# Down projection of an encoder layer: seven products of sums of blocks on half of the row pairs

## The chip, the core and the metric

The kernel runs on one core of a Trainium2 chip. The time is device microseconds (us) of that core for one execution. The engines are TensorE (PE, matrix products, with its weight loads shown as PEld), VectorE (DVE), ScalarE (ACT), GpSimd (POOL) and SyncE (SP). SP issues the transfers of weights here; ACT and POOL can issue transfers too. SBUF is the core's working memory of 128 partitions, PSUM holds the sums of products in 8 banks of 128x512 floats, HBM is the memory outside the core.

## The reference

One layer of an encoder, for one sequence of 256 tokens, model width 2048, inner width 8192, all in float32. Only its last part changes:

```python
    x = x + rms_norm(y, norm_mix_post[l])
    h = rms_norm(x, norm_mlp_pre[l])
    u = jnp.square(jax.nn.relu(jnp.einsum('bsd,df->bsf', h, w_up[l])))
    x = x + rms_norm(jnp.einsum('bsf,fd->bsd', u, w_down[l]), norm_mlp_post[l])
```

The down projection is the second einsum: u (256 x 8192) times w_down (8192 x 2048). Before it come a projection of 10240 columns, two kinds of attention, two branch projections, gates and an output projection, then the up projection, which is the first einsum.

## The kernel before, in words

**Arithmetic.** TensorE works on a 32-bit type that keeps fewer bits than float32. So each operand is split into two parts, high and low: ACT casts the value to the high part, DVE subtracts the high part from the value, which gives the low part. A product is three products on PE: high by high, high by low, low by high.

**Order of work.** The code is written for a scheduler that builds each engine's order from a simulated timeline of all instructions, priorities following the order in which the code is written; `tc.issue_after` adds an order by hand. A buffer is taken from a pool of fixed count; an instruction that needs a buffer waits until the last reader of the tile that held it is done. `pages` has 27 buffers of 4 KB a partition. `wp` has three buffers of 8 KB each for raw weights (tag `raw`), high parts (`hi`) and low parts (`lo`). `tmp` holds temporaries, `mm` and `ms` four PSUM banks each.

**Weights.** `weight` (L119) is `load` (L98, a transfer of 1024 KB on SP's queue) and then `split` (L115 the cast on ACT, L116 the subtraction on DVE, in two pieces of 1024 columns).

**Up projection.** `wgroup` makes 512 columns of u at a time, transposed, in 16 groups. Products are L191 and L192. Each group ends in `u_evac`: `halves` (L254 and L256) adds two halves of a bank, L761 applies relu and the row factor, L762 squares. The groups stay in SBUF as 16 pages `u0` to `u15`.

**Down projection.** It goes over 64 chunks of 128 rows of w_down, each with all 2048 columns. `dweight` (L750) brings a chunk; when a chunk begins a new group of 512 rows, `usplit` (L743 to L747) splits that page of u into `uh` and `ul`. These are the stationaries, the operands that PE holds while a weight chunk streams past. `dmm` (L772 to L780) makes three products of 512 columns, for each of 2 token tiles and 4 column blocks: 24 products a chunk, 1536 in all, into 8 banks `acc` that stay open over the stage:

```python
        nc.tensor.matmul(acc[t][c], uh[:, k % 4, ts_], hi[:, 0, cs], start=(k == 0), stop=False)
        nc.tensor.matmul(acc[t][c], uh[:, k % 4, ts_], lo[:, 0, cs], start=False, stop=False)
```

The last three chunks are done bank by bank. After each bank ACT squares it with a row sum (L807) and DVE multiplies it by the gain (L809). After four banks come the reduction (L811), the inverse root mean square in `inv_rms` (L85 on DVE, L88 a power on POOL), the scaling and the residual (L816), and the transfer out (L819).

## Time and profile before

| | |
|---|---|
| time, median of 3 runs | 1397.59 us (1396.96 to 1397.92) |
| span of the profiled execution | 1394.5 us |
| the median less that span | 3.1 us |
| mean granted TensorE clock | 0.995 |
| the down projection's products | 1536, from 1037.40 to 1385.60 us |
| HBM read, written | 261.92 MB, 3.92 MB |

The profile gives one execution, on the chip. Its own time is the span, from the first to the last instruction. A row of windows reads: the stretch, its length, then the busy time and the count of instructions of PE, PEld, DVE, ACT and POOL, the mean granted PE clock, the mean busy share of the 16 transfer engines and the GB/s they moved. A group's row reads: line, engine, operation, output and inputs, tile shape, count, then busy time and mean ns of one, then the idle time before it and what ended most of that. In the chain of waits a row has a time, a length, the engine and what it worked on.

### The profile page before, as it was taken

To read this page: it belongs to the slowest core of one execution; us is meant where nothing else is said; L and a number is where in the kernel's file an instruction comes from. 1 tells how busy PE (TensorE), PEld (TensorE's weight loads), DVE (VectorE), ACT (ScalarE), POOL (GpSimd) and SP (SyncE) were. 2 spreads that over 40 slices of the span, in tenths; PEclk is the share of its full clock that TensorE was granted. 3 is DMA by queue.
4 is the path that set the end of the run, shared out by engine and by line. 5 is a ranking of instruction groups with operands and counts; after the bars stand their busy time and mean duration, and the time that the engine had idled before them with its cause. 6 is when DMAs were issued, how large, how long until landed. Compare 5 with 4: busy or idle time off the path is not lost.

```text
span 1394.5 us, 17896 instructions
## 1 busy us (share of the span) xinstructions
PE 1374.6 (99%) x7240; PEld 1177.8 (84%) x7240; DVE 835.8 (60%) x1155; ACT 668.7 (48%) x1023; POOL 7.9 (1%) x19
## 2 busy tenths in 40 slices
PE   7999999999999999999899999999999999999997
PEld 6888888888888888888788888888888888888886
DVE  6868866676656565654755555555575554444445
ACT  7554554545444445543744444444464543334332
POOL 0000000000000000000000000000000000000000
PEclk9999999999999999999999999999999999999999
DMA  9674755564555555675455565656555556555551
GB/s 317 202 214 154 202 177 173 171 191 155 165 205 182 203 181 183 203 279 184 149 182 181 182 193 170 211 170 200 189 196 185 203 186 227 195 187 205 181 199 73
DMA packets 117490, 265.16 MB, mean 190 GB/s; under 512 B 15008, under 2 KB 16288, under 8 KB 109216
## 3 DMA queue, kind: packets, MB, share of 16 engines
q1 hardware_dynamic: 117264, 264.03, 57.3%
q8 instruction: 56, 0.92, 0.3%
q14 instruction: 26, 0.21, 0.0%
q10 hardware_dynamic: 144, 0.01, 0.0%
HBM read 261.92 MB, written 3.92 MB: 191 GB/s over the span
## 4 chain that ended last, share of the span: by engine, by line
PE 98%; DVE 1%; DMA 0%; ACT 0%; SPq 0%; issue 0%; DVEq 0%; POOLq 0%; POOL 0%; ACTq 0%
PE u_p L191 17%; PE u_p L192 9%; PE acc L779 8%; PE acc L778 8%; PE acc L777 8%; PE gb_p L191 4%; PE ga_p L191 4%; PE qa_p L191 2%; PE gb_p L192 2%; PE ga_p L192 2%; PE ka_p L191 2%; PE qn_p L191 2%; PE bb_p L191 2%; PE ba_p L191 2%; PE kn_p L191 2%; PE y_p L229 2%
## 5 line engine op out<-in xcount | busy, mean ns | idle before, releaser
L191 PE MATMUL u_p<-h2T,u_h 128*128 128x512 f32 x1024 | 359.9, 398 | 0.5 <-DVE r_m L85 0.5
L192 PE MATMUL u_p<-h2T,u_l 128*128 128x256 f32 x1024 | 284.3, 280 | 0.0
L116 DVE TENSOR_TENSOR d_l<-d_w,d_h 128x1024 fp32r<-128x1024 f32 x128 | 151.1, 1221 | 164.2 <-ACT d_h L115 163.7
L116 DVE TENSOR_TENSOR u_l<-u_w,u_h 128x1024 fp32r<-128x1024 f32 x128 | 151.1, 1222 | 146.0 <-ACT u_h L115 144.7
L191 PEld LDWEIGHTS u_p<-h2T,u_h 128*128 128x128 f32 x1024 | 192.0, 189 | 45.5 <-DVE r_m L85 0.9
L115 ACT CAST d_h<-d_w 128x1024 fp32r<-128x1024 f32 x128 | 128.3, 1052 | 191.1 <-PE acc L779 187.5
L778 PE MATMUL acc<-d_l,uh 128*128 128x512 f32 x512 | 199.0, 389 | 0.0
L779 PE MATMUL acc<-d_h,ul 128*128 128x512 f32 x512 | 198.9, 389 | 0.0
L777 PE MATMUL acc<-d_h,uh 128*128 128x512 f32 x512 | 198.2, 389 | 0.0
L192 PEld LDWEIGHTS u_p<-h2T,u_l 128*128 128x128 f32 x1024 | 193.8, 189 | 1.3
L115 ACT CAST u_h<-u_w 128x1024 fp32r<-128x1024 f32 x128 | 128.0, 1049 | 123.9 <-PE u_p L191 62.5
L778 PEld LDWEIGHTS acc<-d_l,uh 128*128 128x128 f32 x512 | 96.1, 188 | 20.1
L777 PEld LDWEIGHTS acc<-d_h,uh 128*128 128x128 f32 x512 | 96.1, 188 | 20.0
L779 PEld LDWEIGHTS acc<-d_h,ul 128*128 128x128 f32 x512 | 96.1, 188 | 19.8
L191 PE MATMUL gb_p<-hT,gb_h 128*128 128x512 f32 x256 | 90.4, 398 | 0.0
L191 PE MATMUL ga_p<-hT,ga_h 128*128 128x512 f32 x256 | 90.0, 397 | 0.0
L192 PE MATMUL gb_p<-hT,gb_l 128*128 128x256 f32 x256 | 71.4, 281 | 0.0
L192 PE MATMUL ga_p<-hT,ga_l 128*128 128x256 f32 x256 | 70.3, 280 | 0.0
L191 PEld LDWEIGHTS gb_p<-hT,gb_h 128*128 128x128 f32 x256 | 47.9, 188 | 11.5
L116 DVE TENSOR_TENSOR gb_l<-gb_w,gb_h 128x1024 fp32r<-128x1024 f32 x32 | 37.8, 1221 | 31.1 <-ACT gb_h L115 31.1
L191 PEld LDWEIGHTS ga_p<-hT,ga_h 128*128 128x128 f32 x256 | 47.4, 188 | 10.5
L116 DVE TENSOR_TENSOR y_l<-y_w,y_h 128x1024 fp32r<-128x1024 f32 x32 | 37.9, 1222 | 27.8 <-ACT y_h L115 27.8
(213 smaller groups left out, 2348.1 us busy)
## 6 DMA issues: line engine op xcount, KB each, us to landing
u_w<-in_w_up SPq DMA_DIRECT2D x64, 1024.0 KB, 5.4
d_w<-in_w_down SPq DMA_DIRECT2D x64, 1024.0 KB, 4.9
ga_w<-in_w_in SPq DMA_DIRECT2D x16, 1024.0 KB, 5.2
gb_w<-in_w_in SPq DMA_DIRECT2D x16, 1024.0 KB, 5.2
y_w<-in_w_out SPq DMA_DIRECT2D x16, 1024.0 KB, 5.1
ka_w<-in_w_in SPq DMA_DIRECT2D x8, 1024.0 KB, 6.1
va_w<-in_w_in SPq DMA_DIRECT2D x8, 1024.0 KB, 5.2
qn_w<-in_w_in SPq DMA_DIRECT2D x8, 1024.0 KB, 5.1
```

The costliest lines, as they stand in the source:

```text
L115: nc.scalar.copy(hi[part], raw[part])
L116: nc.vector.tensor_sub(lo[part], raw[part], hi[part].bitcast(F32))
L191: nc.tensor.matmul(ps[b], hi[:, k % 4, cs], mv, start=(k == 0), stop=False)
L192: nc.tensor.matmul(ps[b][:, :T], lo[:, k % 4, cs], mv[:, :T], start=False, stop=(k == nk - 1))
L229: nc.tensor.matmul(ps[t], sh, hi[:, k % 4], start=(k == 0), stop=False)
L777: nc.tensor.matmul(acc[t][c], uh[:, k % 4, ts_], hi[:, 0, cs], start=(k == 0), stop=False)
L778: nc.tensor.matmul(acc[t][c], uh[:, k % 4, ts_], lo[:, 0, cs], start=False, stop=False)
L779: nc.tensor.matmul(acc[t][c], ul[:, k % 4, ts_], hi[:, 0, cs], start=False, stop=(k == NK - 1))
```

## The change

**Stage.** The down projection is done in two halves of 1024 output columns each (g = 0 and 1). The 16 groups of 512 rows of w_down are taken in pairs, and a pair makes a block. A group has four chunks of 128 rows; a chunk goes together with its partner 256 rows further down. So a block has four steps, two of each group, and a step's load is again 1024 KB: 128 rows and their partners, 1024 columns (`down_weights`, L818).

**Seven products.** In the even groups (`seven`) a step is a product of 2 x 2 blocks: two token tiles by two chunks, times two chunks by two column blocks. It is made with seven products of blocks and of sums of blocks in place of eight. Each is still three PE products, so a step has 21. The sums of u's blocks are made once a group (`act_sets`), those of the weights' blocks in each step (L833 to L835), and both are split again. Odd groups (`eight`) do the plain eight, 24 PE products. Plain steps add into banks 1, 2, 3 and 7; banks 0, 4, 5 and 6 belong to the seven products alone. They are emptied and combined into `zw` in the last block of a half (L951 to L955), after that block's second seven-product step; the other four banks are added in `rest` (L892). There are 32 steps of 21 products and 32 of 24, 1440 in all.

**Stationaries.** `act_sets` runs behind each group of the up projection, makes the sums and splits all that the group needs, and POOL writes the parts to HBM (48 transfers). `act_again` reads a pair of groups back, one block ahead, by six transfers on ACT's queue (L791). Two pairs are not read again where they are used next: groups 12 and 13 serve the first block of half 0 straight from the up projection, and groups 14 and 15 stay from the last block of half 0 for the first block of half 1.

**The ends of the halves.** A block's steps alternate between its groups: seven-product step s0, plain n0, then s1, n1. The first block of half 0 has n0, s0, s1, n1. The last block of each half has s0, s1, n0, n1, PE's products there stand in the written order, and the two plain steps are done bank by bank: for each bank its products of both steps, then the addition, the square and, in half 1, the gain. Half 0's gains are written in half 1's seventh block.

The diff, from the pools on, with removed code cut where the listing above shows it:

```diff
-    tmp = ctx.enter_context(tc.tile_pool(name="tmp", bufs=6))
+    temps = ctx.enter_context(ExitStack())
+    tmp = temps.enter_context(tc.tile_pool(name="tmp", bufs=6))
...
-    ust = {}
...
+    NG = DFF // 512
+    kept = {}
+    def seven_of(cg):
+        return cg % 2 == 0
+    def act_sets(cg, u):
+        srcs = []
+        if seven_of(cg):
+            a11, a21 = u[:, 0:2, :P], u[:, 0:2, P:]
+            a12, a22 = u[:, 2:4, :P], u[:, 2:4, P:]
+            sums = page([P, 4, 2, P], F32, f"sm{cg}")
+            nc.vector.tensor_sub(sums[:, 0], a21, a22)
+            nc.vector.tensor_sub(sums[:, 1], a11, a21)
+            nc.vector.tensor_sub(sums[:, 2], sums[:, 0], a11)
+            nc.vector.tensor_add(sums[:, 3], a12, sums[:, 2])
+            srcs = [
+                ([P, 3, 2, P], [(slice(0, 1), u[:, 0:2, :P].unsqueeze(1)),
+                                (slice(1, 3), u[:, 2:4].rearrange("p k (t q) -> p t k q", t=2))]),
+                ([P, 4, 2, P], [(slice(0, 4), sums)]),
+            ]
+        else:
+            srcs = [([P, 4, T], [(slice(0, 4), u)])]
+        got = []
+        for i, (shape, pieces) in enumerate(srcs):
+            hi, lo = page(shape, F32R, f"ah{cg}{i}"), page(shape, F32R, f"al{cg}{i}")
+            for at, src in pieces:
+                nc.scalar.copy(hi[:, at], src)
+                nc.vector.tensor_sub(lo[:, at], src, hi[:, at].bitcast(F32))
+            for n, part in (("h", hi), ("l", lo)):
+                kd = dram.tile(shape, F32, name=f"keep{n}{cg}{i}", tag=f"keep{n}{cg}{i}")
+                nc.gpsimd.dma_start(kd, part.bitcast(F32))
+                kept[cg, i, n] = (shape, kd)
+            got.append([hi, lo])
+        return got
+    def act_again(cg, g):
+        out = []
+        for i in range(2 if seven_of(cg) else 1):
+            got = []
+            for n in "hl":
+                shape, kd = kept[cg, i, n]
+                t = page(shape, F32R, f"b{n}{g}{cg}{i}")
+                nc.scalar.dma_start(t.bitcast(F32), kd)
+                got.append(t)
+            out.append(got)
+        return out
+    sets = {}
+    for cg in range(NG):
         u = page([P, 4, T], F32, f"u{cg}")
...
-        uT.append(u)
-        if cg == DFF // 512 - 2:
-            usplit(0)
...
+        got = act_sets(cg, u)
+        if NG - 4 <= cg < NG - 2:
+            sets[0, cg] = got
+    temps.close()
+    down = ctx.enter_context(tc.tile_pool(name="down", bufs=1, reuse_waits="tile"))
+    wd = a["w_down"].rearrange("(g h j p) c -> p h g j c", h=2, j=2, p=P)
...
+    def down_weights(g, cg, j):
+        raw = wp.tile([P, 4, 512], F32, tag="raw", name=f"dr{g}{cg}{j}")
+        last_load[0] = nc.sync.dma_start(
+            raw.rearrange("p (h b) c -> p h (b c)", h=2),
+            wd[:, :, cg, j, g * 1024 : (g + 1) * 1024],
+        ).ins
+        n = f"{g}{cg}{j}"
+        h1, l1 = wtile("hi", f"dh{n}"), wtile("lo", f"dl{n}")
+        if not seven_of(cg):
+            nc.scalar.copy(h1, raw)
+            nc.vector.tensor_sub(l1, raw, h1.bitcast(F32))
+            return h1, l1
+        t = [page([P, 2, 512], F32, f"dt{n}{i}") for i in range(2)]
+        nc.scalar.copy(h1[:, 1:4], raw[:, 1:4])
+        nc.vector.tensor_add(t[0], raw[:, 1:3], raw[:, 0:1].to_broadcast([P, 2, 512]))
+        nc.vector.tensor_add(t[1][:, 0], t[0][:, 0], raw[:, 2])
+        nc.vector.tensor_add(t[1][:, 1], t[1][:, 0], raw[:, 3])
+        nc.vector.tensor_sub(l1[:, 1:4], raw[:, 1:4], h1[:, 1:4].bitcast(F32))
+        h2 = [down.tile([P, 2, 512], F32R, tag="e", name=f"eh{n}{i}", bufs=4) for i in range(2)]
+        l2 = [page([P, 2, 512], F32R, f"el{n}{i}") for i in range(2)]
+        for i in range(2):
+            nc.scalar.copy(h2[i], t[i])
+            nc.vector.tensor_sub(l2[i], t[i], h2[i].bitcast(F32))
+        return h1, l1, h2, l2
+    class Products:
...
+        def add(self, i, stat, w, blk, last=False):
+            (sh, sl), (wh, wl) = stat, w
+            for n, (st, mv) in enumerate(((sh, wh), (sh, wl), (sl, wh))):
+                with tc.issue_after(self.after) if self.after else nullcontext():
+                    ins = nc.tensor.matmul(
+                        self.ps[i], st, mv[:, blk], start=i not in self.begun, stop=last and n == 2
+                    ).ins
+                self.begun.add(i)
+                if self.in_order:
+                    self.after = ins
+    def seven(pr, sets, j, w, last):
+        def stat(i, at):
+            return tuple(part[:, at, j] for part in sets[i])
+        r, t = w[:2], list(zip(*w[2:]))
+        order = [(0, 0, 0, r, 1), (4, 1, 0, t[0], 0), (6, 1, 1, t[0], 1), (5, 1, 2, t[1], 0)]
+        own = [(2, 1, 3, r, 2), (1, 0, 1, r, 3), (3, 0, 2, t[1], 1)]
+        order = order + own if not pr.begun else order[:1] + own[:2] + order[1:] + own[2:]
+        for i, part, at, ww, blk in order:
+            pr.add(i, stat(part, at), ww, blk, last and i in (0, 4, 5, 6))
+    PLAIN = ((1, 0, 1), (2, 0, 0), (3, 1, 1), (7, 1, 0))
+    def eight(pr, sets, j, w, which, last):
+        i, t, half = PLAIN[which]
+        for k in (0, 2):
+            stat = tuple(part[:, j + k, t * P : (t + 1) * P] for part in sets[0])
+            pr.add(i, stat, w, k + half, last and k == 2)
+    zw = {}
+    ssd = [small(4, f"ssd{t}") for t in range(2)]
+    def rest(g, which, pr):
+        i, t, half = PLAIN[which]
+        z = zw[g, t][:, half]
+        nc.vector.tensor_add(z, z, pr.ps[i])
+        sq = down.tile([P, 512], F32, tag="junk", name=f"jd{g}{which}", bufs=2)
+        c = g * 2 + half
+        nc.scalar.activation(sq, z, AF.Square, accum_out=ssd[t][:, c : c + 1])
+    def gain(g, t, half):
+        z = zw[g, t][:, half]
+        nc.vector.tensor_mul(z, z, gp2[g][:, half * 512 : (half + 1) * 512])
+    def finish(t):
         sd = small(1, f"sd{t}")
-        nc.vector.tensor_reduce(sd, ssd, axis=AX.X, op=ALU.add)
+        nc.vector.tensor_reduce(sd, ssd[t], axis=AX.X, op=ALU.add)
         rd = inv_rms(sd, D, f"rd{t}")
...
+    blocks = [[NG - 4] + list(range(0, NG - 4, 2)) + [NG - 2], [NG - 2] + list(range(0, NG - 2, 2))]
+    for g in range(2):
+        pr = Products(f"p{g}", (0, 4, 5, 6))
+        for bi, b in enumerate(blocks[g]):
+            s0, s1, n0, n1 = (b, 0), (b, 1), (b + 1, 0), (b + 1, 1)
+            end = bi == len(blocks[g]) - 1
+            steps = [n0, s0, s1, n1] if g == 0 and bi == 0 else [s0, n0, s1, n1]
+            if end:
+                steps = [s0, s1, n0, n1]
+                pr.in_order = True
+            ws = {}
+            for n, (cg, j) in enumerate(steps):
+                ws[cg, j] = w = down_weights(g, cg, j)
+                if n == 0 and not end:
+                    for c in range(2):
+                        sets[g, blocks[g][bi + 1] + c] = act_again(blocks[g][bi + 1] + c, g)
+                if n == 0 and end and g == 0:
+                    for c in range(2):
+                        sets[1, b + c] = sets[0, b + c]
+                if g == 1 and bi == 5 and n == 0:
...
+                if g == 1 and bi == 6:
+                    gain(0, n // 2, n % 2)
+                if seven_of(cg):
+                    final = end and n == 1
+                    seven(pr, sets[g, cg], j, w, final)
+                    if final:
+                        for t in range(2):
+                            zw[g, t] = page([P, 2, 512], F32, f"zw{g}{t}")
+                        c11, c12 = zw[g, 0][:, 1], zw[g, 0][:, 0]
+                        c21, c22 = zw[g, 1][:, 1], zw[g, 1][:, 0]
+                        nc.scalar.copy(c11, pr.ps[0])
+                        nc.vector.tensor_add(c12, c11, pr.ps[5])
+                        nc.vector.tensor_add(c21, c12, pr.ps[6])
+                        nc.vector.tensor_sub(c12, pr.ps[4], c12)
+                        nc.vector.tensor_sub(c22, pr.ps[4], c21)
+                elif not end:
+                    for which in range(4):
+                        eight(pr, sets[g, cg], j, w, which, False)
+                elif n == 3:
+                    for which in range(4):
+                        for c, jj in (n0, n1):
+                            eight(pr, sets[g, c], jj, ws[c, jj], which, jj == 1)
+                        rest(g, which, pr)
+                        if g:
+                            gain(1, *PLAIN[which][1:])
+                            if which % 2:
+                                finish(which // 2)
```

**Three places in the order of the instructions.** The first is DVE in a steady block, in the middle of the stage. Before, `d` names are weight chunks (11 to 13 here), `_l`, `_h` and `_w` their low part, high part and raw buffer, `ul` low parts of u:

```order
L747 TENSOR_TENSOR ul9_10399<-u9_7879,uh9_10398 128x1024
L116 TENSOR_TENSOR d11_l_9577<-d11_w_9574,d11_h_9576 128x1024 x2
L116 TENSOR_TENSOR d12_l_9613<-d12_w_9610,d12_h_9612 128x1024 x2
L116 TENSOR_TENSOR d13_l_9645<-d13_w_9642,d13_h_9644 128x1024 x2
L747 TENSOR_TENSOR ul10_10531<-u10_8068,uh10_10530 128x1024
```

In the changed kernel, a block of half 1 with groups 6 and 7 (numbers are half, group, chunk, and a last digit for the sum): `dr` are raw weights, `dt` sums, `dh` and `dl` own high and low parts, `eh` and `el` those of the sums:

```order
L833 TENSOR_TENSOR dt1600_11307<-dr160_11303 128x1024
L836 TENSOR_TENSOR dl160_11306<-dr160_11303,dh160_11305 128x1536
L834 TENSOR_TENSOR dt1601_11308<-dt1600_11307,dr160_11303 128x512
L841 TENSOR_TENSOR el1600_11316<-dt1600_11307,eh1600_11314 128x1024
L835 TENSOR_TENSOR dt1601_11308<-dt1601_11308,dr160_11303 128x512
L828 TENSOR_TENSOR dl170_11358<-dr170_11355,dh170_11357 128x2048
L841 TENSOR_TENSOR el1601_11317<-dt1601_11308,eh1601_11315 128x1024
L833 TENSOR_TENSOR dt1610_11389<-dr161_11385 128x1024
L834 TENSOR_TENSOR dt1611_11390<-dt1610_11389,dr161_11385 128x512
```

Where a chunk had two subtractions, a seven-product step has a subtraction of 1536 columns, three sums and two subtractions of 1024; a plain step has one subtraction of 2048. The rows `ul` are gone from the stage.

The second place is DVE in the last block of half 1, with groups 12 and 13; the first seven-product step is `1120`, the second `1121`, the plain ones `1130` and `1131`:

```order
L835 TENSOR_TENSOR dt11201_11772<-dt11201_11772,dr1120_11767 128x512
L836 TENSOR_TENSOR dl1121_11810<-dr1121_11807,dh1121_11809 128x1536
L841 TENSOR_TENSOR el11201_11781<-dt11201_11772,eh11201_11779 128x1024
L833 TENSOR_TENSOR dt11210_11811<-dr1121_11807 128x1024
L828 TENSOR_TENSOR dl1130_11857<-dr1130_11854,dh1130_11856 128x2048
L834 TENSOR_TENSOR dt11211_11812<-dt11210_11811,dr1121_11807 128x512
L841 TENSOR_TENSOR el11210_11820<-dt11210_11811,eh11210_11818 128x1024
L835 TENSOR_TENSOR dt11211_11812<-dt11211_11812,dr1121_11807 128x512
L828 TENSOR_TENSOR dl1131_11863<-dr1131_11860,dh1131_11862 128x2048
L841 TENSOR_TENSOR el11211_11821<-dt11211_11812,eh11211_11819 128x1024
```

Here the two seven-product steps follow one another, and the low part of the first plain step, `dl1130`, stands ahead of the last three sums and parts of the second seven-product step (`dt11211`, `el11210`, `el11211`).

The third place is DVE in the tail. Before, `zw` are the output rows, `acc` the banks, `gp` the gains, `sd` and `rd` the sums of squares and the inverse roots:

```order
L809 TENSOR_TENSOR zw10_11320<-acc10_9210,gp20_11226 128x512
L816 SCALAR_TENSOR_TENSOR zw00_11255<-zw00_11255,rd0_r_11309,x2_0_5443 128x512 x2
L816 SCALAR_TENSOR_TENSOR zw01_11256<-zw01_11256,rd0_r_11309,x2_1_5444 128x512 x2
L809 TENSOR_TENSOR zw10_11320<-acc11_9211,gp20_11226 128x512
L809 TENSOR_TENSOR zw11_11321<-acc12_9212,gp21_11227 128x512
L809 TENSOR_TENSOR zw11_11321<-acc13_9213,gp21_11227 128x512
L811 TENSOR_REDUCE sd1_11370<-ssd1_11319 128x1
L85 TENSOR_SCALAR rd1_m_11372<-sd1_11370 128x1
```

Now, with `p1` and a digit for the banks of half 1:

```order
L892 TENSOR_TENSOR zw10_11847<-zw10_11847,p12_10689 128x512
L899 TENSOR_TENSOR zw10_11847<-zw10_11847,gp21_11487 128x512
L903 TENSOR_REDUCE sd0_11898<-ssd0_9454 128x1
L86 TENSOR_SCALAR rd0_m_11900<-sd0_11898 128x1
L892 TENSOR_TENSOR zw11_11848<-zw11_11848,p13_10690 128x512
L908 SCALAR_TENSOR_TENSOR zw00_10608<-zw00_10608,rd0_r_11902,x2_0_5443 128x512 x2
L908 SCALAR_TENSOR_TENSOR zw10_11847<-zw10_11847,rd0_r_11902,x2_1_5444 128x512 x2
L899 TENSOR_TENSOR zw11_11848<-zw11_11848,gp21_11487 128x512
L892 TENSOR_TENSOR zw11_11848<-zw11_11848,p17_10694 128x512
L899 TENSOR_TENSOR zw11_11848<-zw11_11848,gp21_11487 128x512
L903 TENSOR_REDUCE sd1_11944<-ssd1_9455 128x1
```

The gain reads the output row in SBUF and no longer the bank; each bank costs DVE an addition and a gain. The four scalings of the first token tile stand ahead of the additions' last, that of bank 7.

More of the change, by code (lines that the diff above doesn't have):

```diff
@@ new lines, in encoder_layer, with __init__ @@
+    class Products:
+        def __init__(self, name, low):
+            self.ps = [bank(f"{name}{i}", i in low) for i in range(8)]
+            self.begun = set()
+            self.after = None
+            self.in_order = False
+        def add(self, i, stat, w, blk, last=False):
[8 more added lines that the diff above has]
+                    self.after = ins
@@ L814, in encoder_layer @@
             cs = slice((c % 2) * 512, (c % 2 + 1) * 512)
-            z = zw[c // 2][:, cs]
+            z = zw[c // 2, t][:, c % 2]
             nc.vector.scalar_tensor_tensor(
```

59 lines of the change are left out of this document (8 added, 51 removed).

## The prediction

> **What bounds the kernel now.** First the page's busy shares and its chain of waits: is one engine the bound from end to end?
>
> ```profile
> PE 1374.6 (99%) x7240; PEld 1177.8 (84%) x7240; DVE 835.8 (60%) x1155; ACT 668.7 (48%) x1023; POOL 7.9 (1%) x19
> PE 98%; DVE 1%; DMA 0%; ACT 0%; SPq 0%; issue 0%; DVEq 0%; POOLq 0%; POOL 0%; ACTq 0%
> ```
>
> TensorE (PE) is 99% busy and 98% of the chain that ended last. Then the stages, by a view of windows: an early stretch of full transfers, a stretch of the up projection, the whole down projection, a stretch of it.
>
> ```profile
> 10.00:20.00 10.00, 10.00 (x55) 8.86 (x54) 7.96 (x13) 9.90 (x21) 0.00 (x0) 1.00 1.05 389
> 900.00:1000.00 100.00, 100.00 (x573) 87.15 (x572) 55.45 (x75) 46.93 (x73) 0.00 (x0) 1.00 0.60 189
> 1037.40:1385.60 348.20, 348.17 (x1536) 287.92 (x1535) 172.13 (x154) 143.65 (x157) 0.54 (x1) 1.00 0.54 187
> 1100.00:1200.00 100.00, 100.00 (x443) 82.78 (x442) 50.30 (x43) 40.84 (x41) 0.00 (x0) 1.00 0.58 201
> ```
>
> The third row is the whole stage that changes: 1536 products in 348.20 us, one every 0.2267 us. (The 389 ns that the groups below give for one product is its latency; products overlap.) VectorE (DVE) is busy half of that time, the transfers a little over half. Last, the groups and waits of the stage show who follows whom:
>
> ```profile
> L778 PE MATMUL acc<-d_l,uh 128*128 128x512 f32 x512 | 199.0, 389 | 0.0
> L116 DVE TENSOR_TENSOR d_l<-d_w,d_h 128x1024 fp32r<-128x1024 f32 x128 | 151.1, 1221 | 164.2 <-ACT d_h L115 163.7
> L115 ACT CAST d_h<-d_w 128x1024 fp32r<-128x1024 f32 x128 | 128.3, 1052 | 191.1 <-PE acc L779 187.5 <-issue 3.6
> SPq L98 <- DVE d_l L116: 290.0, 59, 9.1
> ```
>
> PE is idle for 0.0 us ahead of its products. ScalarE (ACT) waits for PE (a buffer of parts), DVE for ACT, the load queue for DVE: everything waits for PE in the end.
>
> **What is removed.** A step is 128 rows of one half of the output columns with their partner rows 256 further down: 24 products, or 21 where the seven-product form is used. 32 of the 64 steps use it: 96 products fewer, 96 x 0.2267 = **-21.8 us**, if PE stays fed. An estimate from the product rate alone, and the whole of the gain.
>
> **What DVE gets.** The trace has no 1536- or 2048-column subtraction; these rows give its slope:
>
> ```profile
> L256 DVE TENSOR_TENSOR up_s<-u_p,up_r 128x256 f32<-128x256 f32 x64 | 25.4, 419 | 0.0
> L809 DVE TENSOR_TENSOR zw<-acc,gp 128x512 f32<-128x512 f32 x8 | 5.3, 688 | 6.2 <-ACT jd L807 5.9
> L371 ACT CAST n_pT<-n_pt 128x512 fp32r<-128x512 f32 x8 | 4.4, 584 | 0.0
> L98 SPq DMA_DIRECT2D d_w<-in_w_down x19: 327/328/328, 1030.1 to 1128.0; - x19
> ```
>
> 419, 688 and 1221 ns lie on 0.154 + 1.043 ns a column, so 1.76 us for 1536 and 2.29 us for 2048. A seven-step costs DVE 1.22 + 2 x 0.69 + 1.76 + 2 x 1.22 = 6.8 us, a plain one 2.3 us. A block (two of each) is 18.2 us of DVE against 90 x 0.2267 = 20.4 us of PE: 89%, where it is 50% now. ACT by 584 and 1052 ns: 1.5 us for 1536, 2.0 for 2048, so 2 x (1.5 + 2.1) + 2 x 2.0 = 11.2 us, and six issues of 0.33 us (SP's issue, the nearest row): 13.2 us, 65%.
>
> In a steady block I followed the order with these durations. ACT may cast a step's high part when PE has read the buffer three steps back; from there low parts and sums are ready about 7 us before PE's turn. The six DMAs on ACT's queue wait for the last use of the sums two blocks back, which lies ahead of the PE product that the next cast waits for: they stop nothing that would run. Cost 0, hidden by those 7 us; without them, what DVE is late.
>
> At three places the cover is thinner. **Start of the stage:** DVE still has the last evacuation and split of the up projection, and takes the sums of both seven-steps after the low part of the fourth step; against PE's 61 products without sums (13.8 us) four waits of 0.4 to 0.9 us come out: 2 us (bounds 0 and 5). **Last block of each half:** the two seven-steps stand together, and the low part of the third step (which needs a buffer that PE leaves only with its last product of the block before) stands ahead of the second seven-step's last parts. From that product: cast 2.0, low part 2.3, sum 0.7, part 1.2, sum 0.7, low part 2.3, part 1.2 = 10.4 us; PE wants the part 37 products later, at 8.4 us (38 in the first half, 8.6). 2 us late, twice: 4 us (bounds 0 and 8). What is late next is the plain steps, whose parts are ready by then. **Change of halves:** banks 0, 4, 5, 6 are emptied under the 48 plain products of that block (10.9 us); DVE has 12.3 us there: 0.5 us (bounds 0 and 3).
>
> **What the transfers get.** Weights are still 64 loads of 1024 KB, now as 4 KB runs. New are the kept stationaries: 2.88 MB a pair of groups (two of 768 columns, four of 1024), written once for eight pairs (23.1 MB, in the up projection) and read for seven pairs in each half (40.4 MB). A steady block reads 4.19 + 2.88 = 7.08 MB in 20.4 us: 347 GB/s. The first window above moved 389 GB/s over 10 us with several transfers in flight: 18.2 us, so it fits. Share against rate gives other ends: 201 / 0.58 = 347 GB/s for the down weights (20.4 us, just even), 189 / 0.60 = 315 for the up weights' 2 KB runs (22.5 us, 2.1 us a block over 14 blocks: +29 us). I take 0, by the row with transfers side by side, and keep +29 as the bound. A load alone lands in
>
> ```profile
> DMA to landing us min/median/max: 4.7/4.9/6.6
> ```
>
> while the steady order leaves the weights 7 to 13 us between issue and first use, plus PE's 7 us; even behind a whole set, (1.05 + 2.88) MB / 389 = 10.1 us and some 2 us, they arrive.
> The Trainium skill (DMA: Bandwidth & Descriptors, Where 436 GB/s comes from) says that for HBM to SBUF a core's share of the HBM, about 358 GB/s, binds. By it a block would take 19.8 us, still under PE's 20.4, with nothing in reserve; this trace disagrees with its 389 GB/s, and the measurement decides.
>
> **Up projection.** A pair of groups (45 us) gets 4 x 0.42 us of sums and 3584 columns of splits: about 5.7 us on DVE and 4 on ACT, from 55% to 68% and 47% to 55%. Its writes raise 189 GB/s to about 253. POOL, idle, issues them; a page is reused a group or more later, 22 us. I take 0. The trace shows no POOL DMA; bounds 0 and +5 (16 groups, a DVE delay of 0.3 us each that reaches PE).
>
> **The tail.**
>
> ```profile
> 1385.34 0.24 PE acc L779
> 1385.66 0.60 ACT jd L807
> 1386.38 0.69 DVE zw L809
> 1388.05 0.75 DVE zw L816
> ```
>
> Now DVE multiplies after the squares, 1.49 us after PE's end. In the change, four scalings of the first token tile (2.74 us) and a gain stand on DVE ahead of the last bank's addition. From the third bank's addition at -2.7 us: 0.7, 2.7, 0.7, then the addition 0.7 ends at 2.1, squares to 2.8, gain to 3.6 us: **+2.1 us** (bounds 0.8, the addition alone, and 3).
>
> **Sum.** The profiled execution has a span of 1394.5 us; with the 3.1 us around it that the median has over the span it stands at the median, 1397.6. 1397.6 - 21.8 + 2 + 4 + 0.5 + 2.1 = **1384.4**, so 1384 us. With the low ends 1376.6, so the floor is 1376.
>
> **Rivals.**
>
> A. The transfers bind (the other side). Place: the 14 blocks that read stationaries; price above 20.4 us a block. At 315 GB/s: 1384 + 29 = 1413. It decides from 331 GB/s (13.6 / 14 = 0.97 us a block eats the gain). For it: the share of the up weights; against it: 389 GB/s at the start, and 4 KB runs that are nearer the 347 row. 0.10.
>
> B. DVE binds in every block. It has 2.2 us to spare a block, 0.55 a step. Its waits for ACT are now
>
> ```profile
> DVE d_l L116 <- ACT d_h L115: 163.7, 57, 3.1
> ```
>
> 2.9 us each, with nothing else to do. If 1 us a step stays, a block takes 22.2 us: 16 x 1.8 = +29, 1413; slower from 0.8 us a step. Against it: in the order each wait has another step's work ahead of it. 0.08.
>
> C. Waits grow long enough to lower PE's clock. Once in this trace PE waited 3.2 us:
>
> ```profile
> PE h2T_t L664 <- DVE x L657: 3.2, 1, 3.2
> 668.00:672.00 4.00, 1.14 (x5) 0.57 (x4) 2.87 (x9) 3.85 (x13) 0.55 (x1) 0.95 0.00 0
> 672.00:676.00 4.00, 3.15 (x10) 2.46 (x11) 3.88 (x12) 3.10 (x8) 0.54 (x1) 0.50 0.00 0
> 676.00:680.00 4.00, 4.00 (x20) 3.58 (x19) 3.82 (x8) 2.85 (x7) 0.00 (x0) 0.69 0.20 32
> ```
>
> and the granted clock was 0.50 and 0.69 in the next 8 us: 2.0 + 1.2 = 3.2 us more. If the start and both last blocks wait 3.2 us instead of 2, it is 3 x (1.2 + 3.2) = +13: 1397. Mine are 2 us, in pieces. 0.10.
> The Trainium skill (TensorE: Matmul & The Clock Gate, What's actually happening) says the clock halves after an idle window of some 3.4 us; the row agrees, and by that rule waits of 2 us cost no clock.
>
> D. PE is fed throughout and only the tail costs: 1397.6 - 21.8 + 2.1 = 1378. DVE's 89% speaks against it. 0.12.
>
> **Chances.** Forecast (1380 to 1391) 0.60, A 0.10, B 0.08, C 0.10, D 0.12. About 0.2%, 2.8 us, is what a measurement of this kernel can tell. Faster by more: forecast, D, and some of C and of mild A or B: 0.81; same 0.07; slower 0.12. The range 1376 to 1397 takes in D and C and leaves out A and B at their prices.
>
> **What would show it.** Right: 1440 products, 0.226 us each in the middle of the stage; PE idle ahead of products some 6 us in all, ended by DVE parts at the start and in the two last blocks; DVE near 0.89 in steady blocks; about 350 GB/s there; 3.6 us from PE's end to the last gain. Wrong: PE waiting for DMA in steady blocks (A), for DVE in each block (B), or a granted clock under 0.99 in the stage (C).

## The result, and the profile after

The changed kernel takes 1389.77 us (median, 1389.23 to 1390.31), the kernel before 1397.53 us beside it. The ratio is 0.9946, with an interval of 0.9934 to 0.9957: 7.8 us faster, where 13.2 were forecast. It lies inside the range of 1376 to 1397. The profiled execution has a span of 1387.3 us, 7.2 less than the 1394.5 of before, so the accounts below go by the spans.

First the page's busy shares and its chain of waits, then the view of PE's waits over the whole span (in all, times, longest):

```profile
PE 1359.3 (98%) x7144; PEld 1162.4 (84%) x7144; DVE 992.9 (72%) x1315; ACT 720.6 (52%) x1041; POOL 34.0 (2%) x67
PE 95%; DVE 2%; DMA 2%; ACT 1%; issue 0%; SPq 0%; DVEq 0%; POOLq 0%; POOL 0%; ACTq 0%
PE p L858 <- ACT dh L832: 2.7, 1, 2.7
PE p L858 <- DVE el L841: 1.7, 1, 1.7
PE p L858 <- ACT eh L840: 1.3, 2, 0.7
PE p L858 <- ACT dh L827: 0.2, 1, 0.2
```

The last four rows, of `p L858`, are the new waits, all in the down projection: 5.9 us, where about 6 were forecast. Only the 1.7 us end with a DVE part, though; the others end with a cast on ACT. PE has 7144 instructions where it had 7240, 96 fewer. Now windows of 20 us through the stage: the start, a steady stretch, the change of halves, another steady stretch and the end.

```profile
1040.00:1060.00 20.00, 18.68 (x82) 14.85 (x81) 17.41 (x17) 9.77 (x11) 1.07 (x2) 1.00 0.76 280
1060.00:1080.00 20.00, 19.76 (x85) 15.39 (x84) 18.26 (x15) 11.32 (x9) 0.00 (x0) 1.00 1.01 391
1140.00:1160.00 20.00, 20.00 (x90) 16.56 (x89) 17.79 (x15) 11.35 (x9) 0.00 (x0) 1.00 0.92 355
1180.00:1200.00 20.00, 17.29 (x69) 13.79 (x68) 16.15 (x14) 8.74 (x8) 0.00 (x0) 0.91 0.59 211
1240.00:1260.00 20.00, 20.00 (x90) 16.57 (x89) 17.34 (x14) 10.49 (x8) 0.00 (x0) 1.00 1.02 398
1360.00:1380.00 20.00, 14.74 (x57) 11.21 (x55) 13.49 (x22) 3.64 (x10) 0.56 (x1) 0.91 0.15 54
```

The two steady windows hold 90 products, as many as before, with DVE at 0.89 and 0.87 and 355 and 398 GB/s; in the others from 1080 to 1180 us and from 1220 to 1340 us DVE lies between 0.76 and 0.94 and the rate between 307 and 378 GB/s, with no wait of PE. So the middle of the stage is what was forecast. The losses sit in the first two windows, at the change of halves and at the end. The last two places have a granted clock of 0.91.

Where the clock went is seen in windows of 2 us and in PE's timeline there (start, length, and in brackets how long PE was idle ahead and what ended it). First the last block of half 1:

```profile
1360.00:1362.00 2.00, 0.83 (x4) 0.21 (x2) 2.00 (x2) 0.75 (x2) 0.00 (x0) 1.00 0.00 0
1362.00:1364.00 2.00, 1.42 (x4) 1.12 (x5) 0.81 (x2) 0.00 (x0) 0.00 (x0) 0.71 0.04 8
1364.00:1366.00 2.00, 2.00 (x7) 1.51 (x6) 1.93 (x4) 0.00 (x0) 0.00 (x0) 0.50 0.00 0
...
1360.33 0.51 PE L858 MATMUL p<-eh,bh 128*128 128x512 f32 x1
1362.58 0.60 PE L858 MATMUL p<-el,bh 128*128 128x512 f32 x1 [1.74 <-DVE el L841]
1362.97 0.63 PE L858 MATMUL p<-eh,bl 128*128 128x512 f32 x1
```

PE waits 1.74 us for the second seven-product step's last low part. From 1360.33 to 1362.58 is 2.25 us for one product, 2.02 us more than its 0.2267. Then products start every 0.43 us, up to 1366.3, while the granted clock is 0.50: 1.70 us more. Together 3.7 us. At the change of halves:

```profile
1192.39 0.50 PE L858 MATMUL p<-eh,bh 128*128 128x512 f32 x1
1195.60 0.80 PE L858 MATMUL p<-dh,bh 128*128 128x512 f32 x1 [2.71 <-ACT dh L832]
1196.19 0.63 PE L858 MATMUL p<-el,bh 128*128 128x512 f32 x1
```

The product at 1195.60 is not of this block. In PE's order a first product of half 1 stands between half 0's sums, and it waits for the cast of half 1's first step. That costs 2.98 us of waiting and 1.69 us of half clock, 4.7 us.

The order of DVE that makes the wait of half 1, in DVE's timeline:

```profile
1354.55 2.29 DVE L828 TENSOR_TENSOR dl<-dr,dh 128x2048 fp32r<-128x2048 f32 x1 [0.98 <-ACT dh L827]
...
1357.36 1.22 DVE L841 TENSOR_TENSOR el<-dt,eh 128x1024 fp32r<-128x1024 f32 x1
1358.50 0.69 DVE L835 TENSOR_TENSOR dt<-dt,dr 128x512 f32<-128x512 f32 x1
1359.10 2.29 DVE L828 TENSOR_TENSOR dl<-dr,dh 128x2048 fp32r<-128x2048 f32 x1
1361.30 1.22 DVE L841 TENSOR_TENSOR el<-dt,eh 128x1024 fp32r<-128x1024 f32 x1
```

Both plain steps' low parts, 2.29 us each, stand ahead of the part that PE wants next. Last, the tail, in the chain of waits:

```profile
1374.48 2.65 DVE zw L908 x4
1377.14 0.60 DVE zw L899
1377.74 0.61 DVE zw L892
1379.18 0.69 DVE zw L899
```

The last product of PE, before and now:

```profile
1385.18 0.39 PE L779 MATMUL acc<-d_h,ul 128*128 128x512 f32 x1
1376.09 0.39 PE L858 MATMUL p<-dh,bl 128*128 128x512 f32 x1
```

So PE ends at 1376.48 now and ended at 1385.57 before. The last bank's addition waits behind four scalings and a gain, and the last gain ends at 1379.87, 3.4 us after PE (3.6 were forecast). From PE's end to the end of the span it is 10.8 us, before 8.9: 1.9 us more.

The account: products -21.8; start +2.9; last block of half 0 +4.7; of half 1 +3.7; tail +1.9; +1.1 that came ahead of the down projection (0.8 of it at the first products of the kernel, which the change doesn't touch, 0.3 later). The sum is -7.5, the spans differ by -7.2; the rest is rounding and gaps of a few hundredths.

### The profile page after: what moved, and what is told of

Its sections match the earlier page's. It is cut to its first block, busy times and chain, and to the rows that moved or that the text cites. A ratio compares the mean times of both kernels' runs of the same rounds, so it can differ in the third digit from the quotient of the medians.

```text
span 1387.3 us, 18177 instructions
## 1 busy us (share of the span) xinstructions
PE 1359.3 (98%) x7144; PEld 1162.4 (84%) x7144; DVE 992.9 (72%) x1315; ACT 720.6 (52%) x1041; POOL 34.0 (2%) x67
## 4 chain that ended last, share of the span: by engine, by line
PE 95%; DVE 2%; DMA 2%; ACT 1%; issue 0%; SPq 0%; DVEq 0%; POOLq 0%; POOL 0%; ACTq 0%
PE p L858 21%; PE u_p L192 17%; PE u_p L193 9%; PE gb_p L192 4%; PE ga_p L192 4%; PE qa_p L192 2%; PE gb_p L193 2%; PE ga_p L193 2%; PE ka_p L192 2%; PE qn_p L192 2%; PE bb_p L192 2%; PE ba_p L192 2%; PE kn_p L192 2%; PE y_p L230 2%; PE y_p L231 2%; PE y_p L232 2%
## 5 line engine op out<-in xcount | busy, mean ns | idle before, releaser
L858 PE MATMUL p<-dl,bh 128*128 128x512 f32 x330 | 129.0, 391 | 0.0
L858 PE MATMUL p<-dh,bl 128*128 128x512 f32 x330 | 128.7, 390 | 0.0
L858 PE MATMUL p<-dh,bh 128*128 128x512 f32 x330 | 117.5, 393 | 2.9 <-ACT dh L832 2.7
L828 DVE TENSOR_TENSOR dl<-dr,dh 128x2048 fp32r<-128x2048 f32 x32 | 73.3, 2290 | 16.1 <-ACT dh L827 16.0
L827 ACT CAST dh<-dr 128x2048 fp32r<-128x2048 f32 x32 | 61.2, 1914 | 41.4 <-DMA dr<-in_w_down 32.4
L840 ACT CAST eh<-dt 128x1024 fp32r<-128x1024 f32 x64 | 66.0, 1048 | 24.5 <-DVE dt L835 12.8
L841 DVE TENSOR_TENSOR el<-dt,eh 128x1024 fp32r<-128x1024 f32 x64 | 77.1, 1219 | 0.0
L858 PEld LDWEIGHTS p<-dh,bh 128*128 128x128 f32 x330 | 62.4, 189 | 16.6 <-ACT dh L832 3.0
L858 PEld LDWEIGHTS p<-dl,bh 128*128 128x128 f32 x330 | 62.4, 189 | 13.9 <-DVE dl L836 0.4
L858 PEld LDWEIGHTS p<-dh,bl 128*128 128x128 f32 x330 | 62.2, 189 | 12.9
```

Source lines behind the costliest of these rows:

```text
L827: nc.scalar.copy(h1, raw)
L828: nc.vector.tensor_sub(l1, raw, h1.bitcast(F32))
L840: nc.scalar.copy(h2[i], t[i])
L841: nc.vector.tensor_sub(l2[i], t[i], h2[i].bitcast(F32))
L858: ins = nc.tensor.matmul(self.ps[i], st, mv[:, blk], start=i not in self.begun, stop=last and n == 2).ins
```

## The experiments

**The order of the low parts in the last blocks.** The main theory was that DVE's order there causes both waits.

```diff
+            with tc.issue_after(low_after) if low_after else nullcontext():
                 nc.vector.tensor_sub(l1, raw, h1.bitcast(F32))
-                ws[cg, j] = w = down_weights(g, cg, j)
+                ws[cg, j] = w = down_weights(g, cg, j, marks[n - 2] if end and n > 1 else None)
```

`marks[0]` is the last of a seven-product step's three sums, `marks[1]` its last low part of a sum.

> Edit: in the last block of each half the low part of the first plain step is ordered behind the second seven-product step's three sums, and the low part of the second plain step behind that step's last low part of a sum. Theory (the waits for the last el, and the half-speed products after them, cost 4.7 us in half 0 and 3.8 us in half 1): both waits go, the granted clock stays at 1.00 to the end of the stage, 1389.8 - 8.5 = 1381.3 us, ratio to the kernel before 0.988. Rival (the lateness only moves on to the plain steps' low parts, or to the load of the first step of half 1, which waits for the same DVE work): half of it at most, about 1385.5 us, and PE waiting for L831 or for a cast of half 1's first step.

Measured: 1380.47 us (1379.87 to 1381.36), ratio to before 0.988, interval 0.9865 to 0.9895. Its window at the change of halves, and PE's waits in the stage:

```profile
1180.00:1200.00 20.00, 20.00 (x90) 16.57 (x89) 18.29 (x18) 9.52 (x10) 0.00 (x0) 1.00 0.62 211
PE p L861 <- ACT eh L843: 1.3, 2, 0.7
PE p L861 <- ACT dh L829: 0.3, 1, 0.3
```

Only the waits at the start are left, and the clock stays at 1.00. The product of half 1 that stood among half 0's sums is behind them in this order too: the edit moved the scheduler's timeline. The two waits and their half clock, 8.4 us by the account, are gone, and the span is 9.2 us shorter (1387.3 to 1378.1; 0.6 us of that lies ahead of the stage): more than the change as given had gained in all. The rival, a lateness that only moves on, falls. In half 1, where no stray product stood, DVE's order was the only cause; in half 0 this edit removes both causes at once, and the next one separates them.

**The stray product alone.** Here half 1's products are ordered behind half 0's last sums, and DVE's order stays.

```diff
-        pr = Products(f"p{g}", (0, 4, 5, 6))
+        pr = Products(f"p{g}", (0, 4, 5, 6), pr.after if g else None)
```

> Edit: the products of half 1 are ordered behind the last product of the second seven-product step of half 0 at least, so that no product of half 1 stands ahead of half 0's last sums (in the changed kernel one does, and waits for a load and a cast of half 1). Theory: the wait in half 0 shortens from 3.0 us of lost time to the 2.0 us that DVE's order costs, the clock still falls to 0.50 behind it as it does in half 1 after a wait of 1.7 us, so 1389.8 - 1.0 = 1388.8 us. Rival (only waits of 3 us and more lower the clock): the 1.7 us of slow products in half 0 go too, 1387.1 us.

Measured: 1388.97 us (1387.03 to 1389.78), which alone can't be told from 1389.77. The trace can: the wait in half 0 is now for DVE, as in half 1.

```profile
PE p L858 <- DVE el L841: 3.5, 2, 1.8
1193.39 0.50 PE L858 MATMUL p<-el,bh 128*128 128x512 f32 x1 [1.76 <-DVE el L841]
```

Both waits cost 2.02 us, and some nine products behind each run at half clock, another 1.7 us. So the stray product had cost 1.0 us, and here a wait of 1.76 us was enough for the clock to fall.

**Which wait lowers the clock.** Six pauses of PE, put into the up projection, show the clock behind waits of several lengths.

```diff
+        if cg in PROBES:
+            pause(PROBES[cg])
```

`pause(n)` is a transpose on PE, n dependent powers on POOL, another transpose that needs them, and then the next group's products.

> Edit: behind groups 1, 3, 5, 7, 9 and 11 of the up projection PE makes a small transpose, waits for a chain of 1, 2, 3, 4, 5 and 7 small powers on POOL, makes another and goes on; nothing is left out. Each power is some 0.55 us, so the waits should be about 0.8, 1.4, 1.9, 2.5, 3.0 and 4.1 us. Theory (in the changed kernel the clock fell after 1.7 us, in the kernel before it did not after 1.2 us): the granted clock is 1.00 behind the first one or two and 0.50 for some 4 us behind all the others, each of which loses 1.7 us beside its wait. Rival (the clock falls only after an idle window of about 3.2 us or more): 1.00 behind the first four as well, 0.50 behind the last one or two. Total by the theory 13.7 us of waits + 4 x 1.7 = about 20 us over 1389.8, by the rival about 16.

Measured: 1416.49 us, one run, some 7 us more than the theory's sum: the last four pauses came out longer than planned. They are 0.70, 1.39, 2.61, 3.75, 4.54 and 6.05 us, 19.0 in all where 13.7 were planned. The ends of the second and the third, and windows there:

```profile
772.55 0.33 PE L811 MATMUL pb<-ident,probe 128*128 128x128 f32 x1 [1.39 <-POOL probe L809]
820.35 0.47 PE L811 MATMUL pb<-ident,probe 128*128 128x128 f32 x1 [2.61 <-POOL probe L809]
...
772.00:774.00 2.00, 1.45 (x9) 1.29 (x10) 1.91 (x2) 1.59 (x4) 0.49 (x1) 1.00 0.70 265
819.00:821.00 2.00, 0.65 (x2) 0.61 (x3) 2.00 (x3) 1.17 (x3) 1.22 (x2) 0.71 0.48 184
821.00:823.00 2.00, 2.00 (x8) 1.66 (x7) 0.79 (x3) 1.11 (x2) 0.00 (x0) 0.50 0.44 79
823.00:825.00 2.00, 2.00 (x13) 1.78 (x12) 1.23 (x1) 0.35 (x1) 0.66 (x2) 0.94 1.00 351
```

Behind 0.70 and 1.39 us the clock stays at 1.00. At all others it falls to 0.50, each time for 3.4 us (1.16 + 2 + 0.24 in the last three rows), for 6.8 us at the longest. So far less than 3.2 us is enough, and the rival falls. But the length of a wait does not settle it. The same kernel also has the late low part in the last block of half 1, and there a wait of 1.76 us leaves the clock at 1.00:

```profile
1391.62 0.50 PE L877 MATMUL p<-el,bh 128*128 128x512 f32 x1 [1.76 <-DVE el L860]
1392.00:1394.00 2.00, 2.00 (x10) 1.65 (x9) 1.47 (x3) 0.00 (x0) 0.00 (x0) 1.00 0.03 8
```

The place of the wait matters too. In all 14 traces the granted clock changes only at points that lie a whole number of steps of 3.41 us apart. Here it falls at 819.84, 871.04, 922.24 and 973.44 us, 15 steps apart each time, wherever the pauses end; in the changed kernel at 1195.57 and 1362.82, 49 steps apart. The changed kernel's wait of 1.74 us lies inside one step. A point at 772.05 cuts the pause of 1.39 us into 0.9 and 0.5, and the wait of 1.76 us above begins at a point. An estimate of PE's idle time in each step (a product counted as 0.2267 us of work, 0.16 us behind its start in the timeline, where the chain of waits puts it) separates the two cases from 60 us on: all 43 steps at full clock with 2.06 us of idle time or more ended in a fall, and none with 2.03 us or less did. This was read from the traces afterwards; no kernel was run to test it.

**The tail.** On top of the moved low parts, two of the first token tile's scalings go ahead of the last addition and two behind it, and the gain writes to another tile, so that it need not wait for the square.

```diff
-        nc.vector.tensor_mul(z, z, gp2[g][:, half * 512 : (half + 1) * 512])
+        return nc.vector.tensor_mul(to, z, gp2[g][:, half * 512 : (half + 1) * 512]).ins
```

> Edit, on top of e1_low: in the tail the gain writes to another tile, so that it need not wait for the square; two of the first token tile's four scalings stand ahead of the last bank's addition and two behind the second inverse root's first operation. Theory (DVE's order, not the transfers out, sets the end behind PE's last product): the last addition starts 1.1 us sooner and the gap of 0.85 us ahead of the last gain goes, 1.2 us less in all: 11.0 us from PE's end to the span's end become 9.8 us, 1379.3 us. Rival (the end is set by the transfers out): 11.0 us stay, 1380.5 us.

Measured: 1379.35 us (1378.73 to 1381.08), ratio to before 0.9874, interval 0.9857 to 0.989. The span is 1377.0, against 1378.1 without the edit. The last addition is no longer the one that waits for scalings:

```profile
1367.09 0.69 DVE L899 TENSOR_TENSOR zw<-zw,p 128x512 f32<-128x512 f32 x1 [0.20 <-PE p L861]
1367.81 0.69 DVE L911 TENSOR_TENSOR zg<-zw,gp 128x512 f32<-128x512 f32 x1
```

From the start of PE's last product to the end of the span it is 10.4 us, with the moved low parts alone 11.2: 0.8 us of the 1.2 expected. The spans differ by 1.1 us, but 0.3 of that lies ahead of the stage. The times agree but can't prove it, since their ranges overlap. This kernel has the lowest median of all those run.

**How much room DVE has.** Two kernels add useless additions of 256 columns to each step, on top of the moved low parts.

```diff
+        nc.vector.tensor_add(filler, filler, raw[:, 0, :256])
```

> Edit, on top of the moved low parts (e1_low, 1380.5 us): in each step DVE makes one more addition of 256 columns, of which nothing uses the result: 0.42 us a step, 1.7 us a block, so that DVE has 18.2 + 1.7 = 19.9 us of work in a block of 20.4 us of PE. Theory (PE stays the bound as long as DVE's work in a block is less than PE's): at most 3 us, at the start of the stage and at its ends, 1380 to 1384 us. Rival (the forecast's rival B: DVE's waits for ACT, 31 us over the changed kernel's stage or 0.5 us a step, have eaten its slack): most of 64 x 0.42 = 27 us shows, 1400 us or more.

Measured: 1409.05 us, one run. The time is the rival's, but the trace does not bear out its reason. These are a row of DVE's waits and a window:

```profile
DVE filler L829 <- DMA dr<-in_w_down: 29.6, 14, 5.2
1300.00:1320.00 20.00, 20.00 (x90) 16.57 (x89) 18.39 (x19) 10.80 (x8) 0.00 (x0) 1.00 0.92 356
```

From 1220 to 1360 us hardly a product is lost (0.2 us in all). Elsewhere the additions stood early in DVE's order and held it until a load landed. So this edit did not measure DVE's room, it added a wait for loads.

> Edit: as e6_dve_1 with two such additions in each step, 0.84 us a step, 3.4 us a block: 21.5 us of DVE for 20.4 us of PE. Theory: DVE binds now, each block waits about 1.1 us, 16 x 1.1 = 18 us, about 1398 us, a little more if the clock falls, with DVE over 0.97 busy in steady blocks and PE's idle time ended by DVE. Rival (what it adds is paid in full): 64 x 0.84 = 54 us, 1434 us. Rival (DVE can run ahead through the buffers): 1381 us.

Measured: 1413.43 us, one run, between the theory's 1398 and the rival's 1434, with 10.4 us of the same waits: it doesn't settle the question either. So the additions were made to read the step's low part, which DVE has itself:

```diff
+        nc.vector.tensor_add(filler, filler, l1[:, 1, :256].bitcast(F32))
```

> Edit: as e6_dve_1 (one more addition of 256 columns a step on DVE, 0.42 us, on top of e1_low), but the addition reads the step's low part, which DVE itself has made, and not the raw weights. In e6_dve_1 the additions stood early in DVE's order and held it until the loads landed (29.6 us of waits in the trace). Theory (steady blocks stay fed while DVE's work is under PE's; e6_dve_1's loss was that wait): 19.9 us of DVE for 20.4 us of PE, no loss in steady blocks, some 3 to 6 us at the start and around the halves' ends, 1383 to 1387 us. Rival (any addition of DVE's work shows in full): 1407 us, with losses in steady blocks too.

> Edit: two such additions a step, 0.84 us: 21.5 us of DVE for 20.4 us of PE in a block. Theory: each steady block waits about 1.1 us for DVE, and the ends some 5 us more: 1380.5 + 16 x 1.1 + 5 = 1403 us, DVE over 0.97 busy. Rival (paid in full): 1380.5 + 54 = 1434 us. The difference to e10_dve_1b by the theory is some 18 us, by the rival 27 us.

Measured: 1385.54 us with one addition, 1394.48 with two (one run each): +5 and +14 over 1380.5. A steady window of the kernel with one addition, then one at the change of halves and a steady one of the kernel with two:

```profile
1300.00:1320.00 20.00, 20.00 (x90) 16.57 (x89) 18.45 (x19) 10.70 (x8) 0.00 (x0) 1.00 0.89 347
```

```profile
1180.00:1200.00 20.00, 15.83 (x67) 12.38 (x66) 19.09 (x23) 11.91 (x10) 0.00 (x0) 0.99 0.67 244
1320.00:1340.00 20.00, 20.00 (x90) 16.57 (x89) 19.97 (x25) 9.32 (x7) 0.00 (x0) 1.00 0.92 354
```

Even at 19.97 of 20 us of DVE the steady block is fed. So the 1403 us expected with two additions were too many. The reason can be read in DVE's timeline above: an operation starts up to 0.09 us before the one ahead of it ends (2.29 us from 1359.10, the next at 1361.30). An estimate from such rows: 14 operations make a block some 17 us of DVE and not 18.2, and two more in each step make it some 19.7, still under PE's 20.4. Of the 16.4 us that PE loses with two additions, 0.9 lie in steady blocks (from 1140 to 1180 us); the rest is lost at the start, at the change of halves and in the last block. So DVE does not bind the steady blocks of the change, and its work matters in the thin places.

**How much room the transfers have.** The first try put two more reads of 512 KB a block into ACT's queue:

```diff
+                    for c in range(2):
+                        read_more((blocks[g][bi + 1] + 3 + 2 * c) % NG, g)
```

> Edit, on top of e1_low: with each pair of stationaries ACT's queue reads two more pages of 512 KB that nothing uses. A block that reads moves 4.19 + 2.88 + 1.05 = 8.1 MB in 20.4 us, 398 GB/s. Theory (the changed kernel's stage shows windows of 400 to 420 GB/s, so that 398 still fits; what it costs is at the start, where PE waited for a late load): 1381 to 1385 us, 90 products in 20 us in most steady blocks. Rival (a ceiling lies at the 355 GB/s that the steady blocks move now; the Trainium skill, DMA: Bandwidth & Descriptors, Where 436 GB/s comes from, gives 358 for a core): a block takes 22.7 us, 14 x 2.3 = 32 us more, 1412 us, with PE's waits ended by casts that wait for loads.

Measured: 1414.45 us, one run, the rival's time. But ACT's waits show its queue:

```profile
ACT dh L834 <- DMA bl<-keepl: 30.3, 5, 6.3
ACT dh L840 <- DMA bh<-keeph: 23.1, 3, 8.1
```

The casts need none of these tiles, and yet waited 53 us in these rows, 67 in all, until transfers of kept parts were done: they stood behind issues in ACT's queue (that the issues waited for pages to come free is argued, not shown). The moved bytes are mixed with a blocked queue, so the extra copies went to POOL's queue, from HBM to HBM, with no page:

```diff
+                    copy_more(w[0], cg)
```

> Edit, on top of e1_low: in each block that reads stationaries POOL's queue copies one more 512 KB part from HBM to HBM, behind a small POOL operation that reads the block's first high part; no buffer of SBUF and no place in ACT's or SP's queue is taken. In e9_more_reads the added reads stood in ACT's queue, and casts waited 53 us in the trace for transfers that were queued ahead of them. Theory (the transfers have room above the 355 GB/s of the steady blocks, since single windows of 400 to 420 GB/s lost no product; e9's loss was ACT's queue): 380 to 405 GB/s in steady blocks and at most 5 us more, 1381 to 1386 us. Rival (the ceiling is about 360 GB/s): a block of 7.6 to 8.1 MB takes 21.1 to 22.6 us, 14 x 0.7 to 2.2 = 10 to 31 us more, 1390 to 1412 us, casts waiting for weights.

Measured: 1385.08 us, one run, +4.6. Windows of it:

```profile
1080.00:1100.00 20.00, 19.09 (x82) 14.96 (x81) 16.68 (x15) 10.16 (x8) 0.29 (x1) 1.00 1.02 409
1320.00:1340.00 20.00, 20.00 (x90) 16.54 (x89) 15.93 (x16) 9.64 (x7) 2.24 (x2) 1.00 1.02 409
```

At 409 GB/s the second window loses no product, nor does the one from 1160 to 1180 us at 406. The first loses 1.7 us at the same rate, and DVE waits 24.4 us for loads in the stage, where it waited 3.5 us in the changed kernel: the weights came later, but seldom too late. So the room is there, and not quite free. A ceiling near 358 GB/s, which the Trainium skill (DMA: Bandwidth & Descriptors, Where 436 GB/s comes from) gives for a core's share of the HBM, is not seen on this lone core: these windows and the changed kernel's own 398 disagree with it, and the measurement decides.

**The seven products left out.** The structure of the change with plain steps only:

```diff
     def seven_of(cg):
-        return cg % 2 == 0
+        return False
```

> Edit, on the changed kernel: no group uses the seven products; all 64 steps do the plain eight (1536 products again), and the output rows start from zero. All the rest of the change stays: halves, kept stationaries (2.1 MB a pair now), bank by bank ends, tail. Theory (the gain is the 96 products alone and the losses inside the stage are DVE's work for the seven products): PE fed throughout, the kernel before plus the tail's 2.1 us, 1399.5 us; against the changed kernel with moved low parts 1380.5 + 21.8 - 2.8 of its losses at the start = 1399.5. Rival (the new structure itself costs or gains, through loads, reads or the up projection): off that by more than 3 us.

Measured: 1426.99 us, one run: 27 us more than expected. Windows of its start and middle, and ACT's waits:

```profile
1080.00:1100.00 20.00, 14.68 (x39) 10.63 (x40) 4.50 (x2) 1.90 (x1) 0.00 (x0) 0.67 0.90 349
1140.00:1160.00 20.00, 20.00 (x90) 16.53 (x89) 7.50 (x4) 7.60 (x4) 0.00 (x0) 1.00 0.81 295
ACT dh L827 <- DMA bh<-keeph: 22.4, 2, 11.3
ACT dh L827 <- DMA bl<-keepl: 12.0, 1, 12.0
```

From 1120 us on it holds 90 products in 20 us. Between 1060 and 1113 us PE loses 25.4 us: ACT's queue issued some 27 reads, of several blocks, with long gaps between them, and the casts, which don't need them, stood behind. (A step takes fewer pages here, which let the scheduler put the reads early; that is argued, not shown.) Without that loss the 1427.0 us would be 1401.6, 2 us over the 1399.5 expected, but that is arithmetic and no run. That the 96 products are the gain therefore rests on the steady windows, not on this run.

**No reads of stationaries.**

```diff
-                        sets[g, blocks[g][bi + 1] + c] = act_again(blocks[g][bi + 1] + c, g)
+                        sets[g, blocks[g][bi + 1] + c] = sets[0, NG - 4 + c]
```

> Edit: the stationaries are never read again; every block uses those of groups 12 and 13 that are in SBUF (the products are of the wrong groups of u, as many and of the same shapes; the writes to HBM stay). Theory (the reads are hidden save at the start of the stage, where a load of weights takes 11 us among them): the waits between 1060 and 1067 us go, 1.1 us, all else stays, with 90 products in 20 us in the steady blocks. Rival (transfers contend everywhere and make DVE's and ACT's inputs late, which the last blocks' waits come from): those waits shrink too, by 2 us or more each.

Measured: 1388.57 us, one run. The order of the whole stage changed with it: up to 1077 us PE loses 3.4 us where 2.9 were lost, a wait for a cast became one for a low part (0.4 us), half 0's last block lost 6.0 us and half 1's none. Only the first is an answer: without the reads the start is no shorter, so the late load there is not worth 1.1 us by itself. For the last blocks it is inconclusive.

## Why the prediction was right, and where it was not

The way, the cause and the size within its range were right; the gain was 5.4 us less than forecast, 4.4 us of that in one step. By its steps:

- **96 products, -21.8 us.** Right: 90 products in 20 us in every kernel's windows in which PE isn't kept waiting.
- **DVE and ACT in a steady block.** Right: DVE 0.87 to 0.94 from 1080 to 1180 us (0.89 forecast), and no wait of PE there. Rival B is refuted, and the two kernels with additions show that there was room; the sum of 18.2 us a block was some 1 us too large, since DVE's operations overlap a little.
- **Transfers, 0.** Right: 307 to 398 GB/s in the windows of the steady blocks without a loss. Rival A is refuted.
- **Start, +2.** It was 2.9, inside its bounds of 0 to 5: two waits for casts of sums, then a load that took 11 us among the reads of kept stationaries, which the forecast did not have. It expected DVE parts to end these waits; casts on ACT ended them. What the late load adds stays open, since the kernel without reads loses as much there.
- **Tail, +2.1.** It was 1.9, by the mechanism given.
- **Last blocks, +4 in all.** This step failed by size: 8.4 us. The wait for the low part was forecast at 2 us and measured 2.02 in half 1, with the two low parts ahead as described. Two things were missed. The half clock behind it added 1.7 us in each half. And the stray product of half 1 in PE's order made half 0's wait 1.0 us longer. It stands in PE's order of instructions; there the forecast followed the order of DVE.
- **Change of halves, +0.5.** No loss of its own: with the low parts moved, the window from 1180 to 1200 us holds 90 products.
- **Rival C** was given 0.10, on the ground that waits of 2 us in pieces leave the clock alone. That was the wrong ground. It came true at two places of its three: about 3.4 us of clock where the price was 13, and a mean clock of 0.99 in the stage, at the edge of the sign given. That both waits lay inside one step of the clock was bad luck: the same wait of half 1 in the kernel with pauses cost 2.1 us and not 3.7. The Trainium skill (TensorE: Matmul & The Clock Gate, What's actually happening) puts the fall of the clock behind an idle window of some 3.4 us; the prediction saw it agree with a wait of 3.2 us, but no row then showed a wait between 1.2 and 3.2. The waits of 1.74 and 1.76 us that lowered the clock here disagree with it, and the measurement decides.
- **Rival D**, nothing but the tail, is refuted by the 11.3 us lost inside the stage.

The rest of the difference is the 1.1 us ahead of the stage, of which 0.8 lies where both kernels are the same. The forecast had no term for it.

## What to carry to other kernels

When a change takes work off the bound engine, count the waits at its ends one by one, and read the order of both engines there: PE's queue as well as that of the engine that feeds it. Give a wait of PE two prices, its length alone and its length with the half clock behind it; here 2.0 us of lateness cost 3.7 us at three places and 2.1 at a fourth. In this kernel a busy share of 0.89, or even 0.98, of the feeding engine did no harm in the steady blocks, while operations placed too early in DVE's order, or transfer issues that waited ahead of a cast in ACT's, cost 25 us and more.

## What was not expected of the hardware

PE's clock fell to 0.50 at waits of 1.74 to 1.76 us, once stayed at 1.00 at one of 1.76, and changed only at points whole steps of 3.41 us apart; it was low for 3.4 us, and for 6.8 at the wait of 6.05. A lone core moved 406 to 409 GB/s over 20 us while PE ran at its full pace.
